# A list-scheduled two-layer encoder: other lengths for the loading queue in the plan

## The chip, the cores and the metric

The kernel runs on one core of one Trainium2 chip. The time is that of one execution on the device, in microseconds (us), the median of several runs. A core has TensorE (PE), VectorE (DVE), ScalarE (ACT), GpSimd (POOL) and SyncE (SP); SP only issues loads and copies. GpSimd and SP each have a queue of transfers, q0 and q1 in the profile, and 16 DMA engines serve both.

## The reference

A hybrid encoder of two layers in float32, 512 tokens of width 1024, feed-forward width 2816. Each layer runs four steps, every one closed by a layer norm:

```python
x = LN(alpha * x + 0.5 * swiglu(x, w_gate, w_up, w_down))   # first half feed-forward
x = LN(alpha * x + mixer_i(x))                              # token mixing
x = LN(alpha * x + mem_cross_attention(x, mem))             # 4 heads into 256 memory tokens
x = LN(alpha * x + 0.5 * swiglu(x, w_gate, w_up, w_down))   # second half feed-forward

def swiglu(x, w_gate, w_up, w_down):
    return (jax.nn.silu(x @ w_gate) * (x @ w_up)) @ w_down
```

mixer_0 (mixer_ab here) is one projection into two groups of heads, dense attention with rotary positions and attention in a window of 128 with a sink, and one output projection with ab_w_out. mixer_1 (mixer_c) is attention in a two-dimensional neighbourhood with a bias.

## The kernel before

Everything stays on the core from start to end: x is held as four tiles of 128 tokens (x0 to x3), and transposed as xh and xl for the matmuls. A product in float32 is made of three matmuls. Each operand is split into a high part (a cast on ScalarE) and a low part (a subtraction on VectorE), and high x high, high x low and low x high are added up in one PSUM bank. So a weight goes through four hands: a load of 512 KB or 1 MB on SP's or GpSimd's queue, a cast on ScalarE, a subtraction on VectorE, then matmuls on TensorE. In the trace "CAST slab<-slab" and "TENSOR_TENSOR slab<-slab,slab" are these two.

The stages follow each other: ffn0 (to about 330 us), mixer_ab (530), memory (750), ffn1 (1050), ffn2 (1390), mixer_c (1600), memory (1810), ffn3 (2130). The feed-forward steps go in groups of 512 hidden columns. In the groups that this text speaks of, the weights w_gate and w_up come in quarters and some products are taken of sums of quarters, which VectorE makes ("slab<-slab,slab ... f32<-"), so that a group needs fewer matmuls and more of VectorE.

The order of the instructions is not written by hand. The kernel's code is recorded as a graph of `Op` objects (`record`, from L138), each with an estimated time `ns`. `plan` (L181) plays the graph through a model of the five engines: at each step the engine that can start earliest takes its most urgent ready operation. Two lists in it, `queues`, model the loads: `begin`, `finish` and `lands` say when the first packet goes, when the last one has gone, and when readers may start. `plan` is called twice by `emit` (L298): from the first pass `deadlines` works out how late each operation may be, these become the keys of the second pass, and the operations are issued in the order of that pass.

Buffers are handed out in the same pass. Tiles of the kind slab share 27 buffers (t2: 14, raw: 2). A new tile gets the buffer that came free first in the model (`free`, a heap by time), and waits on the chip for the readers of the tile that had it before. The names in the orders below carry running numbers: slab_375 is a tile, not a buffer.

All instructions are issued by one helper line, L156, so every row of the profile names L156 (L157 after the change).

Of the kernel before, what the change touches and what calls it, by code (L numbers as in the profile page):

```python
# [39 lines left out]

class Op:
    __slots__ = (
        "engine", "adds", "ns", "call", "deps", "users", "wait", "ready", "end", "frees", "index", "rank", "dma", "size", "port", "table",
        "key", "start", "stop", "lands", "later",
    )

# [19 lines left out]
class Graph:  # L66
# [71 lines left out]
    def record(self, engine, method, args, kw):  # L138
        kw = dict(kw)
        aps = [z for z in list(args) + list(kw.values()) if hasattr(z, "tensor")]  # L140
        outs = [kw[k] for k in ("out", "accum_out") if k in kw]
        if "out" not in kw:
            outs.insert(0, args[0])
        ins = [z for z in aps if not any(z is o for o in outs)]
        op = Op()
        op.engine, op.index, op.dma, op.adds = engine, len(self.ops), method == "dma_start", "accum_op" in kw
        op.rank = op.index
        op.ns = self.cost(engine, method, outs[0], ins, kw)
        func = args[2] if method == "activation" else None
        op.table = str(func) if func in (AF.Silu, AF.Exp) else None  # L150
        op.size = math.prod(outs[0].shape) * 4
        op.port = method in ("tensor_tensor", "scalar_tensor_tensor", "tensor_scalar") and (
            engine == "gpsimd" or engine == "vector" and math.prod(outs[0].shape[1:]) >= 64 and all(z.space != bass.MemoryType.PSUM for z in ins)
        )
        fn = getattr(getattr(self.nc, engine), method)
        op.call = lambda: fn(*args, **kw)  # L156
        op.deps, op.users, op.frees, op.later = set(), [], [], []  # L157
        if self.after and engine in self.after[1]:
            op.deps.add(self.after[0])
        for z, writes in [(z, False) for z in ins] + [(z, True) for z in outs]:  # L160
            info = self.tiles.get(z.tensor.name)
            if info is None:
                continue
            p0, p1, runs = self.extent(z)
            opens = writes and kw.get("start", False)
            keep = []
            for q, w, a0, a1, other in info["log"]:
                over = opens or p0 < a1 and a0 < p1 and (
                    info["bank"] and q.engine != engine or any(l < b and a < h for l, h in runs for a, b in other)
                )  # L170
                if over and (w or writes or info["bank"] and q.engine != engine) and q is not op:
                    op.deps.add(q)
                covered = writes and p0 <= a0 and a1 <= p1 and all(any(l <= a and b <= h for l, h in runs) for a, b in other)
                if not covered:
                    keep.append((q, w, a0, a1, other))
            keep.append((op, writes, p0, p1, runs))
            info["log"] = keep
            info["users"].add(op)
        self.ops.append(op)

    def plan(self):  # L181

        for info in self.tiles.values():
            info["left"], info["at"], info["behind"] = len(info["users"]), 0.0, None
        now = {e: 0.0 for e in self.ENGINES}
        heaps = {e: [] for e in self.ENGINES}
        ready = {e: [] for e in self.ENGINES}
        free = {s: [(0.0, i, None) for i in range(s.bufs)] for s in self.spaces.values()}
        turn = {s: 0 for s in free}
        queues = {True: [(0.0, 0.0)], False: [(0.0, 0.0)]}  # L190
        held, order, table = [0.0, 0.0], [], None
        for op in self.ops:
            op.wait, op.ready = len(op.deps) + len(op.frees), 0.0

        def release(op, t):
            op.ready = max(op.ready, t)
            op.wait -= 1
            if op.wait == 0:
                heapq.heappush(heaps[op.engine], (op.ready, op.key, op.index, op))

        def grant(space):

            while turn[space] < len(space.queue) and free[space]:
                info = space.queue[turn[space]]
                turn[space] += 1
                if info["users"]:
                    t, _, info["behind"] = heapq.heappop(free[space])
                    for op in info["users"]:
                        release(op, t)

        def arrive(e):
            while heaps[e] and heaps[e][0][0] <= now[e]:
                _, key, i, op = heapq.heappop(heaps[e])
                heapq.heappush(ready[e], (key, i, op))

        for op in self.ops:
            if op.wait == 0:
                heapq.heappush(heaps[op.engine], (0.0, op.key, op.index, op))
        for space in free:
            grant(space)  # L220
        while len(order) < len(self.ops):
            best = None
            for e in self.ENGINES:
                arrive(e)
                if ready[e] and e in self.PATIENT:
                    key, _, op = ready[e][0]
                    for at, k, _, _ in heapq.nsmallest(4, heaps[e]):
                        if at < now[e] + op.ns * 0.6 and k < key - self.margin:
                            now[e] = at
                            arrive(e)  # L230
                            break
                if ready[e]:
                    t = now[e]
                elif heaps[e]:
                    t = heaps[e][0][0]
                else:
                    continue
                if best is None or t < best[0]:
                    best = (t, e)
            assert best, "no instruction can start"  # L240
            t, e = best
            if not ready[e]:
                now[e] = t
                continue
            _, _, op = heapq.heappop(ready[e])
            shared = lambda pairs, a, b: sum(max(0.0, min(b, y) - max(a, x)) for x, y in pairs)
            stop = t + op.ns
            if op.port:
                stop += max(0.0, held[e == "vector"] - t)
                held[e != "vector"] = stop  # L250
            if op.table and op.table != table:
                stop += 1290.0
                table = op.table
            lands = stop + self.LATENCY[e]
            if op.dma:
                kind = e == "sync"
                work = op.size / 2**19 * (4000.0 if op.adds else 1650.0)
                begin = max(stop + (1200.0 if kind else 2000.0), queues[kind][-1][1])
                finish = begin + work + 0.5 * shared(queues[not kind][-6:], begin, begin + work)
                queues[kind].append((begin, finish))  # L260
                lands = finish + 790.0
            op.start, op.stop, op.lands, now[e] = t, stop, lands, stop
            order.append(op)
            for u in op.users:
                release(u, stop if e == u.engine == "tensor" else lands)
            for info in op.frees:
                info["left"] -= 1
                info["at"] = max(info["at"], lands)
                if info["left"] == 0:
                    heapq.heappush(free[info["space"]], (info["at"], len(order), info))  # L270
                    grant(info["space"])
        return order
# [1388 lines left out]
```

## Time and profile before

| | us |
|---|---|
| median of three runs | 2132.85 |
| lowest and highest run | 2131.11, 2132.93 |
| profiled execution | 2131.03 |
| its span | 2129.3 |
| TensorE busy in it | 2112.0 |
| VectorE, ScalarE, GpSimd busy | 1735.8, 1161.7, 285.1 |

The granted clock of TensorE is 0.998 over the span. A row of the timeline has its start, its length, the engine, the line, the operation with the tiles that it writes and reads (without their numbers), how many instructions it sums up, and in brackets the idle time before it with what ended it. "PE" rows are matmuls; "a", "d" and "t" are PSUM banks, slab, raw and t tiles in the core's memory.

### The profile page before, as it was taken

The numbers are of one execution on the slowest core, as the hardware profiler recorded it, in microseconds if no ns is written. First come the engines' busy times: TensorE is split into PE (matmuls) and PEld (weight loads), VectorE is DVE, ScalarE is ACT, GpSimd is POOL, SyncE is SP. The second block draws the span as 40 slices with busy tenths as digits, with TensorE's granted clock in tenths as the row PEclk, the third lists the DMA queues.
The fourth block names the chain that finished last, engine by engine and source line by source line (L and its number), as shares of the span: only waits on it lengthen the run. The fifth ranks groups of instructions, "written<-read, shape, count | busy, mean of one in ns | idle before, by whom it ended". The sixth has DMA issues, their size and how long they took to land.

```text
span 2129.3 us, 32714 instructions
## 1 busy us (share of the span) xinstructions
PE 2112.0 (99%) x12648; PEld 1870.6 (88%) x12648; DVE 1735.8 (82%) x2500; ACT 1161.7 (55%) x1903; POOL 285.1 (13%) x379
## 2 busy tenths in 40 slices
PE   9999999999999999999999999999999999999997
PEld 7999988888888899998889999888888888999996
DVE  7789989888848879998879999866568479699997
ACT  5555443798546554445545455457665465444552
POOL 0001015310002000000200000312210011000003
PEclk9999999999999999999999999999999999999999
DMA  6566562003433346564445556256454433456551
GB/s 204 143 165 140 139 191 91 20 18 106 140 134 109 88 114 185 150 157 130 140 106 141 129 139 187 76 149 160 118 164 157 139 91 98 109 149 155 141 151 60
DMA packets 208859, 275.92 MB, mean 130 GB/s; under 512 B 10688, under 2 KB 151616, under 8 KB 208704
## 3 DMA queue, kind: packets, MB, share of 16 engines
q1 hardware_dynamic: 175904, 221.14, 33.6%
q0 software_dynamic: 32512, 52.44, 14.0%
q8 instruction: 100, 1.64, 0.3%
q14 instruction: 55, 0.45, 0.1%
q10 hardware_dynamic: 288, 0.26, 0.0%
HBM read 259.12 MB, written 4.19 MB: 124 GB/s over the span
## 4 chain that ended last, share of the span: by engine, by line
PE 89%; DVE 1%; DMA 1%; ACT 1%; issue 1%; SPq 0%; DVEq 0%; POOL 0%; ACTq 0%
PE a L156 55%; PE d L156 21%; PE t L156 14%; DMA slab<-t 1%; ACT slab L156 1%; DVE slab L156 1%; SPq L156 0%; DVE x L156 0%; ACT t L156 0%; DMA raw<-ab_w_out 0%; DVE t L156 0%; DVE xl L156 0%; DVEq L1657 0%; ACT xh L156 0%; DVE nmu L156 0%
## 5 line engine op out<-in xcount | busy, mean ns | idle before, releaser
L156 DVE TENSOR_TENSOR slab<-slab,slab 128x1024 fp32r<-128x1024 f32 (+3 forms) x638 | 727.9, 1167 | 76.0 <-ACT slab L156 37.7
L156 ACT CAST slab<-slab 128x1024 fp32r<-128x1024 f32 (+2 forms) x498 | 472.1, 983 | 341.4 <-DVE slab L156 142.7
L156 PE MATMUL a<-slab,slab 128*128 128x256 f32 (+3 forms) x2320 | 567.6, 323 | 1.9 <-DMA slab<-t 1.2
L156 PE MATMUL a<-xh,slab 128*128 128x256 f32 (+2 forms) x2480 | 559.8, 315 | 0.1
L156 PE MATMUL d<-slab,slab 128*128 128x512 f32 (+2 forms) x1856 | 447.8, 381 | 0.8 <-DVE slab L156 0.8
L156 PEld LDWEIGHTS a<-slab,slab 128*128 128x128 f32 x2320 | 409.4, 190 | 41.7 <-ACT t L156 1.3
L156 PEld LDWEIGHTS a<-xh,slab 128*128 128x128 f32 x2480 | 416.4, 190 | 33.4 <-ACT slab L156 1.0
L156 PE MATMUL a<-raw,slab 128*128 128x256 f32 x2048 | 388.8, 283 | 1.1 <-DVE t L156 1.0
L156 PE MATMUL a<-xl,slab 128*128 128x256 f32 (+1 forms) x1240 | 389.7, 314 | 0.0
L156 PEld LDWEIGHTS d<-slab,slab 128*128 128x128 f32 x1856 | 328.9, 189 | 57.2 <-DVE slab L156 1.7
L156 PEld LDWEIGHTS a<-raw,slab 128*128 128x128 f32 x2048 | 327.8, 192 | 6.7 <-ACT slab L156 1.9
L156 PEld LDWEIGHTS a<-xl,slab 128*128 128x128 f32 x1240 | 236.3, 191 | 18.4
L156 PE MATMUL t<-slab,slab 128*128 128x512 f32 (+1 forms) x840 | 209.3, 389 | 0.0
L156 DVE TENSOR_TENSOR slab<-raw,slab 128x1024 fp32r<-128x1024 f32 (+2 forms) x140 | 159.6, 1157 | 23.3 <-ACT slab L156 23.2
L156 PEld LDWEIGHTS t<-slab,slab 128*128 128x128 f32 x840 | 149.9, 189 | 26.2
L156 DVE TENSOR_TENSOR slab<-t,slab 128x512 fp32r<-128x512 f32 (+2 forms) x223 | 137.5, 637 | 12.3 <-ACT slab L156 11.2
L156 ACT CAST slab<-t 128x512 fp32r<-128x512 f32 (+2 forms) x223 | 120.7, 567 | 41.4 <-DVE t L156 15.0
L156 ACT CAST slab<-raw 128x1024 fp32r<-128x1024 f32 (+1 forms) x132 | 123.7, 970 | 25.1 <-PE a L156 9.0
L156 ACT COPY t<-a 128x512 f32<-128x512 f32 (+1 forms) x116 | 63.5, 551 | 130.0 <-PE a L156 76.5
L156 DVE SCALAR_TENSOR_TENSOR x<-d,x 128x512 f32<-128x512 f32 x168 | 114.9, 686 | 16.8 <-PE d L156 16.1
L156 POOL DMA_DIRECT2D slab<-ffn_w_down x40 | 47.7, 1193 | 315.2 <-DVE slab L156 296.9
L156 DVE TENSOR_TENSOR t<-a,t 128x512 f32<-128x512 f32 (+2 forms) x99 | 61.0, 618 | 33.8 <-PE a L156 20.6
(126 smaller groups left out, 2143.0 us busy)
## 6 DMA issues: line engine op xcount, KB each, us to landing
slab<-ffn_w_gate SPq DMA_DIRECT2D x80, 512.0 KB
slab<-ffn_w_up SPq DMA_DIRECT2D x80, 512.0 KB
slab<-ffn_w_down SPq DMA_DIRECT2D x80, 512.0 KB
slab<-ffn_w_down POOLq DMA_DIRECT2D x40, 512.0 KB, 5.8
raw<-mem_w_kv SPq DMA_DIRECT2D x16, 1024.0 KB
slab<-t SPq DMA_DIRECT2D x96, 128.0 KB
slab<-ffn_w_gate POOLq DMA_DIRECT2D x16, 512.0 KB, 7.7
slab<-ffn_w_up POOLq DMA_DIRECT2D x16, 512.0 KB, 6.0
```

What stands on the lines that cost most here:

```text
L156: op.call = lambda: fn(*args, **kw)
```

## The change

Only the planner's model of the loading queue is changed. A load on SP's queue of size bytes had a length of 1650 ns for each 512 KB; now it is 250 ns + 1700 ns for each 512 KB. Its first packet came 1200 ns after the end of the issue (`stop`), and the issue is modelled with a length of its own; now it comes 1040 ns after the start of the issue (`t`). A load of at least 512 KB on at most 64 partitions is marked `thin`, and its length is multiplied by 1.7: only the four pieces of ab_w_out for raw_1188 and raw_1193 are such. The accumulating loads on GpSimd's queue keep 4000 ns for each 512 KB, and other loads there 1650 ns.

```diff
@@ record
+        op.thin = op.dma and engine == "sync" and op.size >= 2**19 and outs[0].shape[0] <= 64
...
@@ plan
             if op.dma:
                 kind = e == "sync"
-                work = op.size / 2**19 * (4000.0 if op.adds else 1650.0)
-                begin = max(stop + (1200.0 if kind else 2000.0), queues[kind][-1][1])
+                work = 250.0 + op.size / 2**19 * 1700.0 if kind else op.size / 2**19 * (4000.0 if op.adds else 1650.0)
+                work *= 1.7 if op.thin else 1.0
+                begin = max(t + 1040.0 if kind else stop + 2000.0, queues[kind][-1][1])
                 finish = begin + work + 0.5 * shared(queues[not kind][-6:], begin, begin + work)
                 queues[kind].append((begin, finish))
                 lands = finish + 790.0
```

The instructions are the same; their order on the engines and the buffers of some tiles change. Three places, before and after; the bracket at the end of a row names the semaphores that it waits for.

VectorE in ffn0, at 113 us in the trace of before (slab_260 is a load, slab_217 a product for the next activation):

```order
L156 TENSOR_TENSOR slab_263<-slab_256,slab_262 128x1024 [waits DMAHW5_49,PE_49,Activation_49]
L156 TENSOR_TENSOR slab_266<-slab_265,slab_260 128x1024 [waits DMAHW6_49,DVE_49]
L156 TENSOR_TENSOR slab_217<-t_118_199,t_72_153 128x512
L156 TENSOR_TENSOR t_186_267<-slab_218,slab_217 128x512 [waits DVE_49]
L156 TENSOR_TENSOR t_187_268<-t_186_267,slab_217 128x512 [waits DVE_49]
L156 TENSOR_TENSOR slab_270<-slab_266,slab_269 128x1024 [waits PE_49,Activation_49]
```

The same rows of VectorE after the change:

```order
L157 TENSOR_TENSOR slab_263<-slab_256,slab_262 128x1024 [waits DMAHW5_49,PE_49,Activation_49]
L157 TENSOR_TENSOR slab_217<-t_118_199,t_72_153 128x512 [waits DVE_49]
L157 TENSOR_TENSOR slab_266<-slab_265,slab_260 128x1024 [waits DMAHW6_49,DVE_49]
L157 TENSOR_TENSOR t_186_267<-slab_218,slab_217 128x512 [waits DVE_49]
L157 TENSOR_TENSOR t_187_268<-t_186_267,slab_217 128x512 [waits DVE_49]
L157 TENSOR_TENSOR slab_270<-slab_266,slab_269 128x1024 [waits PE_49,Activation_49]
```

slab_217 has moved ahead of slab_266, the row that waits for a load (DMAHW6).

TensorE at the end of mixer_ab, at 527 us. slab_1189 to slab_1192 are the halves of one piece of ab_w_out (raw_1188), slab_1194 to slab_1197 those of the last piece (raw_1193); d_1199, a_1200 and d_1208 are the banks of three blocks of tokens:

```order
L156 MATMUL d_1199<-slab_1192,slab_1107 128x512
L156 MATMUL d_1199<-slab_1191,slab_1107 128x512
L156 MATMUL d_1199<-slab_1194,slab_1159 128x512 [waits Activation_49]
L156 MATMUL d_1199<-slab_1195,slab_1159 128x512 [waits DVE_49]
L156 MATMUL d_1199<-slab_1194,slab_1159 128x512
L156 MATMUL d_1199<-slab_1196,slab_1184 128x512 [waits Activation_49]
L156 MATMUL a_1200<-slab_1192,slab_1107 128x512
L156 MATMUL d_1199<-slab_1197,slab_1184 128x512 [waits DVE_49]
L156 MATMUL d_1199<-slab_1196,slab_1184 128x512
```

The same place on TensorE after the change:

```order
L157 MATMUL d_1199<-slab_1192,slab_1107 128x512
L157 MATMUL d_1199<-slab_1191,slab_1107 128x512
L157 MATMUL a_1200<-slab_1192,slab_1107 128x512
L157 MATMUL a_1200<-slab_1191,slab_1107 128x512
L157 MATMUL d_1208<-slab_1189,slab_1047 128x512 [waits DVE_49]
L157 MATMUL d_1199<-slab_1194,slab_1159 128x512 [waits Activation_49]
L157 MATMUL a_1200<-slab_1194,slab_1159 128x512
L157 MATMUL d_1208<-slab_1190,slab_1047 128x512
L157 MATMUL d_1208<-slab_1189,slab_1047 128x512
L157 MATMUL d_1208<-slab_1191,slab_1107 128x512
L157 MATMUL d_1208<-slab_1192,slab_1107 128x512
L157 MATMUL d_1199<-slab_1195,slab_1159 128x512 [waits DVE_49]
```

Matmuls of the other two blocks with the earlier piece (a_1200, d_1208) have moved ahead of and between those of d_1199 with the last piece.

SP's queue in a group of ffn0, from 156 to 184 us, and ScalarE at 179 us. slab_375 is the first quarter of the next group's w_up; this place recurs ten times over ffn0 to ffn3:

```order
L156 DMA slab_351<-ffn_w_down 128x2x512 [waits DMASW3_49,PE_49]
L156 DMA slab_367<-ffn_w_down 128x2x512 [waits DMAHW3_49,DVE_49,PE_49]
L156 DMA slab_375<-ffn_w_up 128x4x256 [waits DMAHW4_49,DVE_49,PE_49]
L156 DMA slab_378<-ffn_w_up 128x4x256 [waits DMAHW6_49,DMAHW5_49,DVE_49]
L156 DMA slab_379<-ffn_w_up 128x4x256 [waits DMAHW3_49,DVE_49]
```

ScalarE at the same place before:

```order
L156 COPY t_260_341<-a_346 128x512 [waits DVE_49,Activation_49]
L156 COPY t_261_342<-a_352 128x512 [waits PE_49]
L156 CAST slab_368<-slab_332 128x1024 [waits DMAHW6_49]
L156 CAST slab_371<-slab_367 128x1024 [waits DMAHW3_49,DVE_49,Activation_49]
L156 CAST slab_373<-slab_314 128x512 [waits PE_49]
```

SP's queue there after the change:

```order
L157 DMA slab_351<-ffn_w_down 128x2x512 [waits PE_49]
L157 DMA slab_367<-ffn_w_down 128x2x512 [waits DMAHW3_49,DVE_49,PE_49]
L157 DMA slab_375<-ffn_w_up 128x4x256 [waits DMASW5_49,DMAHW4_49,DVE_49,PE_49]
L157 DMA slab_378<-ffn_w_up 128x4x256 [waits DMAHW6_49,DMAHW5_49,DVE_49]
L157 DMA slab_379<-ffn_w_up 128x4x256 [waits PE_49]
```

ScalarE there after the change:

```order
L157 COPY t_260_341<-a_346 128x512 [waits DVE_49,Activation_49]
L157 CAST slab_368<-slab_332 128x1024 [waits DMAHW6_49,PE_49]
L157 COPY t_261_342<-a_352 128x512 [waits PE_49]
L157 CAST slab_371<-slab_367 128x1024 [waits DMAHW3_49,DVE_49,Activation_49]
L157 CAST slab_373<-slab_314 128x512 [waits PE_49]
```

On SP the loads keep their order. slab_375 has got another buffer, with a wait more (DMASW5, a load of long before), and its wait on PE is now for the last reader of slab_344, not of slab_349. On ScalarE the cast slab_368 and the copy of a_352 have changed places.

More of the change, by code (lines that the diff above doesn't have):

```diff
@@ L42 @@
     __slots__ = (
-        "engine", "adds", "ns", "call", "deps", "users", "wait", "ready", "end", "frees", "index", "rank", "dma", "size", "port", "table",
+        "engine", "adds", "ns", "call", "deps", "users", "wait", "ready", "end", "frees", "index", "rank", "dma", "size", "port", "table", "thin",
         "key", "start", "stop", "lands", "later",
```

## The prediction

> **What bounds the kernel now.** I read the page first, then the list of what TensorE waits for, then the timelines of each engine around every wait, and last the DMA queues in short windows. TensorE's row says nearly all:
>
> ```profile
> span 2129.3 us, 32714 instructions
> PE 2112.0 (99%) x12648; PEld 1870.6 (88%) x12648; DVE 1735.8 (82%) x2500; ACT 1161.7 (55%) x1903; POOL 285.1 (13%) x379
> ```
>
> TensorE is idle for 2129.3 - 2112.0 = 17.3 us. The change keeps all 12648 matmuls, so it can only move what lies in these 17.3 us. Where they lie:
>
> ```profile
> 2116.00:2129.30 13.30, 2.35 (x11) 1.59 (x9) 8.59 (x14) 1.24 (x2) 3.67 (x4) 0.74 0.50 158
> ...
> PE t L156 <- DVE junk L156: 1.2, 1, 1.2
> PE a L156 <- DMA slab<-t: 1.2, 3, 0.6
> ```
>
> The first row is the last 13.30 us, in which TensorE is busy for 2.35: 10.95 us are the end of the program (last normalisation and store), whose order on TensorE does not change. 1.2 us is the start. So 17.3 - 10.95 - 1.2 = 5.1 us are left in the middle, and that is the most that any order could bring back there. Adding idle time has no such limit.
>
> **The change part by part.** It removes and adds no instruction; it gives the planner other times for loads on SP's queue, and so moves rows on all five queues and hands some buffers to other tiles. I compared the two orders on each engine and went to each moved piece in the trace of before.
>
> *A wait in ffn0 at 129.8 us.* VectorE's row order changes at 113.8:
>
> ```profile
> 113.81 1.23 DVE L156 TENSOR_TENSOR slab<-slab,slab 128x1024 f32<-128x1024 f32 x1 [1.49 <-DMA slab<-ffn_w_down]
> 114.95 0.69 DVE L156 TENSOR_TENSOR slab<-t,t 128x512 f32<-128x512 f32 x1
> ...
> 123.15 2.96 DVE L156 TENSOR_TENSOR slab<-slab,slab 128x1024 fp32r<-128x1024 f32 x3 [0.20 <-ACT slab L156]
> ...
> 128.97 0.69 DVE L156 TENSOR_TENSOR t<-a,t 128x512 f32<-128x512 f32 x1
> ```
>
> ```profile
> 127.22 1.55 PE L156 MATMUL t<-slab,slab 128*128 128x512 f32 x6
> 129.80 0.36 PE L156 MATMUL a<-raw,slab 128*128 128x256 f32 x1 [1.03 <-DVE t L156]
> ```
>
> VectorE idles 1.49 us for a load (slab_266 reads slab_260), then runs almost without a gap to the t whose end at 129.66 lets TensorE go on at 129.80. The new order puts the 0.69 us product slab_217 into that idle time, ahead of the waiting instruction. All behind it comes up to 0.7 us sooner; the 0.20 of waiting for ScalarE at 123.15 may eat some. TensorE's wait is 1.03, so what goes is 0.65 (between 0 and 0.9), and what is late next is the same t, with 0.4 left.
>
> *The end of mixer_ab.* These weights are the ones on 64 partitions.
>
> ```profile
> 526.26 1.96 PE L156 MATMUL d<-slab,slab 128*128 128x512 f32 x7
> 528.98 0.98 PE L156 MATMUL d<-slab,slab 128*128 128x512 f32 x3 [0.76 <-DVE slab L156]
> ```
>
> ```profile
> 512.66 0.61 ACT L156 ACTIVATE t<-t,mn 128x385 f32<-128x385 f32 x1
> ...
> 514.14 1.19 ACT L156 CAST slab<-t 128x256 fp32r<-128x256 f32 x3 [0.28 <-PE t L156]
> ...
> 516.08 2.19 ACT L156 CAST slab<-raw 128x512 fp32r<-128x512 f32 x4
> ...
> 526.61 2.00 ACT L156 CAST slab<-raw 128x1024 fp32r<-128x1024 f32 x2 [1.98 <-DMA raw<-ab_w_out]
> ```
>
> The casts at 526.61 wait for the last piece of ab_w_out, VectorE's difference follows, and TensorE stops 0.76 us at d_1199<-slab_1195. Shown idle time starts at the modelled end of a matmul. Two 512-column matmuls in a row take 0.62 (the row at 374.57 further down) and six 1.55 (127.22), so one starts every (1.55 - 0.62) / 4 = 0.23 and lasts 0.39: against that pace the wait costs 0.76 + 0.39 - 0.23 = 0.92. Two things change. Between d_1199<-slab_1194 and d_1199<-slab_1195 now stand five other matmuls, and three more ahead of the first: 8 x 0.23 = 1.84 us more work, which covers the 0.92 alone. And the four casts of mem_t (516.08) move up to 512.66, three ahead of slab_1167's cast and the fourth soon behind, so that the buffer of raw_1193 comes free sooner. Against it: three of them take 3/4 of 2.19 = 1.64, so the cast that began at 514.14 begins at 514.31 at the earliest, and with what stands behind it TensorE meets two or three just-in-time casts later than before. I take +0.2 for that (0 to 0.6). Sum: -0.7, between -1.2 and -0.3.
>
> *mixer_c at 1530 us.* The "DMA slab<-t" in the list of waits is mostly this:
>
> ```profile
> 1529.53 0.25 PE L156 MATMUL a<-slab,slab 128*128 128x192 f32 x1
> 1530.38 0.33 PE L156 MATMUL a<-slab,slab 128*128 128x192 f32 x1 [0.60 <-DMA slab<-t]
> ```
>
> The first and second half of a_2886 stood back to back; the new order puts eight other matmuls between them, and at the 0.12 to 0.23 us of their pace that is over 1 us of work, so the wait of 0.60 goes. But the subtraction that frees the buffer of load raw_2909 now stands behind two more rows of VectorE, so that load is issued up to 1 us later, and these copies are behind it on SP's queue. The next matmul on that path (a_2892) gets VectorE's maximum behind a longer subtraction. I take -0.4 (-0.7 to +0.3).
>
> *mixer_ab at 374 us.* Here a wait is added:
>
> ```profile
> 368.38 0.74 POOL L156 TENSOR_TENSOR slab<-t,t 128x256 f32<-128x256 f32 x1
> ...
> 373.43 2.39 POOL L156 TENSOR_TENSOR slab<-t,t 128x512 f32<-128x512 f32 x1 [1.30 <-DVE t L156]
> ```
>
> ```profile
> 374.57 0.62 PE L156 MATMUL a<-slab,xh 128*128 128x512 f32 x2
> ```
>
> The transpose t_673 reads what GpSimd ends at 373.43 + 2.39 = 375.82. It stood eight matmuls further on and now stands at 374.57. GpSimd's 0.74 us product at 368.38 has moved behind the chain that feeds this, so the end comes at about 375.08: TensorE waits 0.5 us, with everything queued behind it (0 to 1.25, the upper end if GpSimd is no sooner).
>
> *The quarter loads of w_up.* Ten times (ffn0 to ffn3) the load of the first up quarter gets another buffer: not that of slab_349, last read by the matmul that ends at 179.74, but that of slab_344, last read five 512-column matmuls later. SP holds it for 5 x 0.23 = 1.15 us more, so it issues at 180.9 instead of:
>
> ```profile
> 179.77 4.33 SPq L156 DMA_DIRECT2D slab<-ffn_w_up  x3
> ```
>
> ```profile
> 185.51 1.05 ACT L156 CAST slab<-slab 128x1024 fp32r<-128x1024 f32 x1 [0.88 <-DMA slab<-ffn_w_up]
> ```
>
> ```profile
> 187.16 1.22 DVE L156 TENSOR_TENSOR slab<-slab,slab 128x1024 fp32r<-128x1024 f32 x1
> 188.30 0.69 DVE L156 TENSOR_TENSOR t<-a,t 128x512 f32<-128x512 f32 x1
> ```
>
> ScalarE waits for that landing, so at first sight this moves the path. The queues say otherwise. The next rows are bytes by queue, q0 GpSimd's and q1 SP's, in 180.9 to 183.1, in 183.6 to 187.4, and, at the last of the ten places, in 2017.8 to 2020.0:
>
> ```profile
> q0 software_dynamic: 190, 0.39, 107.3%
> ...
> q1 hardware_dynamic: 1383, 1.38, 108.2%
> ...
> q0 software_dynamic: 209, 0.43, 107.0%
> ```
>
> Until 183.1 not one packet of SP's moves: all 16 DMA engines are full with the down weights that GpSimd issued here:
>
> ```profile
> 178.37 1.20 POOL L156 DMA_DIRECT2D slab<-ffn_w_down  x1 [4.88 <-DVE slab L156]
> ```
>
> When nothing is in the way, the first packet comes 1.0 us after the issue (a load issued at 1742.96, forty slices of 0.1 us from there):
>
> ```profile
> 1742.96 0.37 SPq L156 DMA_DIRECT2D slab<-ffn_w_gate  x1
> ...
> DMA  0000000000873463689999999999888876978989
> ```
>
> An issue at 180.9 is ready at 181.9 and still waits until 183.1. The landing stays, and I cost the edit at 0. Its cover is the rest of the GpSimd transfer, 1.2 us; without it the whole 1.15 would come through.
>
> [...]
>
> *All other moved rows* (three matmuls at the start, single swaps in mixer_c and the layer starts, loads issued 1 to 2 us later whose readers come over 1.5 us after the landing): +0.2, between -0.5 and +1.0.
>
> Sum: -0.65 - 0.7 - 0.4 + 0.5 + 0 + 0.2 = -1.05 us. The profiled execution took 2131.03 (span 2129.3 and 1.7 around it), so it would take 2130.0. It is near the lowest of the three runs, 2131.11; the median is 2132.85, and from that the forecast is 2131.8.
>
> **The rivals.** *The up quarters land late, and it is slower.* If SP's packets do get in between, each of the ten landings is up to 1.15 later. At the first place VectorE (187.16) starts 0.60 after the cast ended (185.51 + 1.05), and its t (188.30 to 188.99) is 0.49 early for the matmul that reads it:
>
> ```profile
> 189.48 0.28 PE L156 MATMUL a<-raw,slab 128*128 128x256 f32 x1
> ```
>
> There 1.15 - 0.60 - 0.49 = 0.1 comes through. At the last place nothing is left over: the cast ends 2024.59, VectorE starts 0.03 later, and TensorE already starts late.
>
> ```profile
> 2023.54 1.05 ACT L156 CAST slab<-slab 128x1024 fp32r<-128x1024 f32 x1 [2.06 <-DMA slab<-ffn_w_up]
> ```
>
> ```profile
> 2024.62 1.23 DVE L156 TENSOR_TENSOR slab<-slab,slab 128x1024 fp32r<-128x1024 f32 x1 [0.53 <-ACT slab L156]
> ```
>
> There all 1.15 does. Ten places between 0.1 and 1.15, half-way 0.63: +6.3, so 2131.8 + 6.3 = 2138.1. It decides from the point where SP issues later than 183.1 - 1.0 = 182.1, and the new issue is 1.2 us short of that; or where the GpSimd transfer ends that much sooner. Against it stand the two windows without one SP packet. *The gains are given back.* TensorE pulled ahead by 0.7 meets its next just-in-time tile sooner; with 99% busy there are many such places. Then 129.8 and 528.98 shift instead of going, the added 0.5 at 374 and 0.2 elsewhere stay: 2132.85 + 0.7 = 2133.6. *The new times for loads do nothing useful*, rows merely swap: 2132.85; this counts with the second. *All goes well*: every middle wait that is touched vanishes, nothing is added: -0.9 - 1.2 - 0.7 - 0.5 = -3.3, 2129.6.
>
> **How the numbers follow.** My forecast, a small gain with its terms near the values taken, 0.55. Given back or nothing, 0.28. Late up quarters, 0.10. All well or better, 0.04; some load or buffer that I did not see and that costs over 4 us, 0.03. 0.2% of 2132.85 is 4.27 us, about what a measurement of this kernel can tell from no change; all cases but the late quarters and the unseen one lie within it. Faster by that much would need nearly all of the 5.1 us: 0.03. Slower: 0.10 of the late quarters and 0.02 of the unseen: 0.12. Within: 0.85. The range goes from the best sum, 2129.6, less 0.3 for the scatter of the runs, 2129.3, up past the second rival and half of the terms' upper ends to 2135.6, and leaves the slower rival out.
>
> **What would show it.** In the profile after: TensorE's wait near 129.8 at about 0.4; none at d_1199<-slab_1195; none for slab<-t near 1530; a new one of 0.5 for GpSimd near 374.6; the up quarters issued 1.15 later after their matmuls and landing, against the GpSimd transfer, at the same time; busy time unchanged at 2112. I am wrong if the idle sum leaves 14.5 to 19 us, or if ScalarE's cast near 185.5 comes a microsecond later and TensorE waits behind it ten times.

## The result, and the profile after

The changed kernel takes 2127.38 us (median of 11 runs, 2125.79 to 2128.19) against 2132.05 (11 runs, 2129.83 to 2133.01): a ratio of 0.9978, 95% interval 0.9970 to 0.9986. It is faster by about 4.7 us, where 2131.8 was forecast and 2129.3 was the low end of the range. The two profiled executions stand at 2131.03 and 2126.97. The page after:

```profile
span 2125.2 us, 32740 instructions
PE 2110.4 (99%) x12648; PEld 1870.4 (88%) x12648; DVE 1736.4 (82%) x2500; ACT 1161.4 (55%) x1903; POOL 288.0 (14%) x379
```

TensorE's idle time fell from 17.3 to 14.8 us, by 2.5, and its busy time from 2112.0 to 2110.4, by 1.6. The matmuls are the same, so I take the second part as waiting too, counted as busy where the modelled end of a matmul lies behind the next start (a 512-column matmul is shown 0.39 long, and in a run one starts every 0.23). The lateness below, taken from the starts alone, falls by 4.11, as much as both parts together. The end of the program is what it was (15.20 - 4.24 = 10.96 us idle, as before 10.95):

```profile
2110.00:2125.20 15.20, 4.24 (x19) 3.10 (x17) 10.25 (x15) 2.37 (x4) 4.37 (x4) 0.74 0.44 139
```

What TensorE still waits for (total, times, longest):

```profile
PE t L157 <- DVE junk L157: 1.2, 1, 1.2
PE t L157 <- DVE x L157: 0.8, 2, 0.7
PE a L157 <- DMA slab<-t: 0.6, 2, 0.3
PE a L157 <- DVE slab L157: 0.4, 1, 0.4
```

VectorE's wait at 129.8 and its subtraction at 528.98 are off the list. The three waits for copies "slab<-t" (1.2) are gone as well; the two now listed (0.6) stand at other places, 0.32 at 1458.74 and 0.25 at 1503.80. To see where the 4 us went I summed TensorE's *lateness*: for each matmul the time from its start to the next start, less the pace that rows of its width keep in a run (0.227 us for 512 columns, 0.120 for 256, 0.113 for 192). It has no modelled end in it. A stretch is cut at the same counts of matmuls in each kernel and is named by its time in the kernel before:

```
stretch, us              before   after
0 to 100 (start)           2.68    2.48
100 to 150 (ffn0)          1.44    0.26
150 to 490                 5.11    5.26
490 to 579 (mixer_ab)      2.54    1.69
579 to 1475               7.66    7.48
1475 to 1607 (mixer_c)     4.67    2.95
1607 to the last matmul    2.60    2.47
sum                       26.71   22.60
```

Three stretches carry 3.75 of 4.11 us. In ffn0 VectorE's product now fills the idle time and, in addition, the load behind it is there at once:

```profile
112.56 0.68 DVE L157 TENSOR_TENSOR slab<-t,t 128x512 f32<-128x512 f32 x1
113.16 1.22 DVE L157 TENSOR_TENSOR slab<-slab,slab 128x1024 f32<-128x1024 f32 x1
...
127.58 0.69 DVE L157 TENSOR_TENSOR t<-a,t 128x512 f32<-128x512 f32 x1
```

The t that TensorE waited for starts at 127.58 instead of 128.97 (the prediction shows the rows of before). At the end of mixer_ab the matmuls run on where the wait of 0.76 stood, with a small new one 8 us later:

```profile
527.68 1.75 PE L157 MATMUL d<-slab,slab 128*128 128x512 f32 x7
...
536.18 1.09 PE L157 MATMUL t<-ident,x 128*128 128x128 f32 x8 [0.18 <-DVE x L157]
```

In mixer_c two waits for copies that the prediction did not show stood in the kernel before (0.44 and 0.51 lost against the pace, less of it shown):

```profile
1482.86 0.58 PE L156 MATMUL a<-slab,slab 128*128 128x192 f32 x3 [0.28 <-DMA slab<-t]
...
1552.90 0.33 PE L156 MATMUL a<-slab,slab 128*128 128x192 f32 x1 [0.30 <-DMA slab<-t]
```

They are gone, and so is the one at 1530. Where the first stood, the rows after run without a gap, and the new wait comes 24 us later:

```profile
1479.60 0.86 PE L157 MATMUL a<-slab,slab 128*128 128x192 f32 x6
1480.29 1.46 PE L157 MATMUL d<-slab,slab 128*128 128x256 f32 x10
...
1503.80 0.33 PE L157 MATMUL a<-slab,slab 128*128 128x192 f32 x1 [0.25 <-DMA slab<-t]
```

### The profile page after: what moved, and what is told of

Read it like the earlier page. It is cut to its first block, busy times and chain, and to the rows that moved or that the text cites. A ratio compares the mean times of both kernels' runs of the same rounds, so it can differ in the third digit from the quotient of the medians.

```text
span 2125.2 us, 32740 instructions
## 1 busy us (share of the span) xinstructions
PE 2110.4 (99%) x12648; PEld 1870.4 (88%) x12648; DVE 1736.4 (82%) x2500; ACT 1161.4 (55%) x1903; POOL 288.0 (14%) x379
## 3 DMA queue, kind: packets, MB, share of 16 engines
q8 instruction: 100, 1.64, 0.3%
## 4 chain that ended last, share of the span: by engine, by line
PE 97%; DVE 1%; DMA 1%; ACT 1%; issue 0%; SPq 0%; POOL 0%; DVEq 0%; ACTq 0%
PE a L157 59%; PE d L157 23%; PE t L157 15%; DVE x L157 0%; DMA slab<-t 0%; DVE slab L157 0%; DMA raw<-mem_w_kv 0%; SPq L157 0%; ACT slab L157 0%; ACT t L157 0%; DMA raw<-x_t 0%; DVE t L157 0%; ACT xh L157 0%; ACT junk L157 0%; POOL lny L157 0%
## 5 line engine op out<-in xcount | busy, mean ns | idle before, releaser
L157 ACT ACTIVATE t<-a 128x512 f32<-128x512 f32 (+3 forms) x65 | 36.3, 559 | 89.7 <-PE a L157 89.7
```

## The experiments

Times below stand beside runs of the kernel before on the same chip. Their intervals are about 0.0009 of the time to each side, 1.9 us, so single pieces of about 1 us are read from the lateness of one profile of each kernel. Lateness scatters as well: in the seven kernels whose rows in mixer_c are those of before it is 3.97 to 5.89, mean 4.94; in the three with the new rows 2.55 to 3.29, mean 2.93. In ffn0 the twelve with the old rows have 1.13 to 1.64, mean 1.37.

**Early half, late half.** The new lengths hold only on one side of a time in the plan:

```diff
+                new = t < 1390e3
+                work = 250.0 + op.size / 2**19 * 1700.0 if kind and new else op.size / 2**19 * (4000.0 if op.adds else 1650.0)
+                work *= 1.7 if op.thin and new else 1.0
+                begin = max((t + 1040.0 if new else stop + 1200.0) if kind else stop + 2000.0, queues[kind][-1][1])
```

> The new model of the loading queue only while the planner's clock is below 1390 us, so the orders up to the end of ffn2 are those of the changed kernel and the rest is as before. Theory (the gain is a sum of local ones, each where a wait of TensorE goes, and what is won stays won): TensorE's lateness against a steady pace falls by 1.2 in 100 to 150 us and by 0.9 in 500 to 550, and the time by 2.1 us in all (ratio 0.9990), about half of the whole change's 4.07. Rival 1 (what is won early is given back at the next tile that comes just in time, and only mixer_c's part counts): the early waits go and others grow behind them, time within 0.5 us of before. Rival 2 (one place opens the way for all, the early lead makes the later waits go): about the whole 4 us, the waits at 1482 to 1553 smaller although their order is unchanged.

Measured: 2130.07 beside 2131.73, ratio 0.9992 (0.9984 to 1.0001). ffn0 0.84, the end of mixer_ab 1.30 (-0.60 and -1.24), mixer_c 5.26. Its profile also has a wait of 1.1 at 1365 that other kernels with the old rows show or don't show; the last section shows the same wait in another kernel. The two gains are local, and rival 2 is out: mixer_c is no better with its old rows. Rival 1 is not excluded by this run alone. The 1.1 and the 0.6 more in mixer_c offset the gains, so that the sum over the profile is that of before (26.5 beside 26.7), and the interval of the time includes no change; both offsets also occur in kernels with the old order.

The other half has the same edit with `t >= 1390e3`.

> The complement: the new model only from 1390 us on, so mixer_c, ffn3 and the end stand in the new order and all ahead of them as before. Theory (local and additive): the waits near 1482.9, 1485.1, 1530.4, 1552.3 and 1552.9 go, one of about 0.4 appears near 1505, and the time falls by 2.0 us (ratio 0.9991), although the prediction had put only -0.4 there. Rival 1 (only mixer_c's part counts): -4. Rival 2 (the early lead makes the later waits go): these waits stay, and the time is within 0.5 us of before.

Measured: 2130.77, ratio 0.9994 (0.9985 to 1.0003). mixer_c falls to 3.29, all five waits named are gone (two others, 1.1 in all, stand at 1572 and none at 1505), and ffn0 (1.38) and mixer_ab (2.52) are as before. By the lateness the late half brings its share without the early lead, so the two halves are separate gains; the median alone (-1.0, with 1.9 to each side) would not show it. The prediction had all of mixer_c at -0.4 and +0.2.

**Which of the three numbers.** Only the line with 1.7:

```diff
                 work = op.size / 2**19 * (4000.0 if op.adds else 1650.0)
+                work *= 1.7 if op.thin else 1.0
```

> Of the three parts of the change only the factor of 1.7 for large loads on 64 partitions. Its order differs from that before only at the end of mixer_ab. Theory: TensorE's wait at d_1199<-slab_1195 near 529 goes, lateness in 500 to 550 us falls by 0.9 (a wait of up to 0.3 may come a few us later), the time by 0.8 us (ratio 0.9996). Rival (the gain there comes from the loads ahead of it that the other two parts moved): the wait stays, 0 +- 0.3.

Measured: 2130.23, ratio 0.9992 (0.9984 to 1.0001). The wait at d_1199 is gone and the lateness at the end of mixer_ab is 0.93 instead of 2.54, which is more than the theory had. And the change without that line:

> The change without the factor of 1.7: the sooner first packet and the longer transfers only. Its order is that of the changed kernel except at the end of mixer_ab. Theory: all of the gain but that at the end of mixer_ab, so 4.07 - 0.8 = 3.3 us less than before (ratio 0.9985), and a wait of 0.7 to 1.0 near 528 that the changed kernel does not have. Rival (the factor brings most): within 1 us of before.

Measured: 2128.74, ratio 0.9983 (0.9975 to 0.9992); mixer_ab 2.39, ffn0 0.18, mixer_c 2.55. The wait is back:

```profile
527.72 0.97 PE L157 MATMUL d<-slab,slab 128*128 128x512 f32 x3 [0.71 <-DVE slab L157]
```

So the factor of 1.7 makes the gain in mixer_ab, and the other two numbers together make the rest; no run takes these two apart.

**ffn0, one row.** On VectorE alone:

```diff
- slab_266<-slab_265,slab_260 128x1024
  slab_217<-t_118,t_72 128x512
+ slab_266<-slab_265,slab_260 128x1024
```

> Before, with one row moved: VectorE's product slab_217 ahead of the sum slab_266 that waits for a load, in ffn0. Theory (the product fills the idle time, and all behind it comes up to 1.3 us sooner, less what the load's own landing differs): TensorE's wait at 129.8 falls from 1.2 to between 0 and 0.6, time -0.9 us (ratio 0.9996). The prediction's step: -0.65, a wait of 0.4 to 0.5 left. Rival (the wait goes through other rows that the change moved, such as loads): 0, the wait stays at 1.0 or more.

Measured: 2131.67 beside 2132.66, ratio 0.9994 (0.9985 to 1.0003); ffn0 0.89, the wait left is

```profile
129.67 0.36 PE L157 MATMUL a<-raw,slab 128*128 128x256 f32 x1 [0.48 <-DVE t L157]
```

That is the "0.4 left" of the prediction: its step holds, in this one profile, for the row that it looked at. In that kernel the load of slab_260 lands 7.66 us after its issue (before 7.69), in the changed kernel 6.79. Four swaps more, as in the change:

```diff
 VectorE
- slab_232<-slab_170,slab_231
  slab_233<-slab_127,slab_233
+ slab_232<-slab_170,slab_231
- slab_245<-slab_234,slab_244
  slab_246<-slab_234,slab_235
+ slab_245<-slab_234,slab_244
...
 ScalarE: the casts slab_231 and slab_269 one row later
```

> Before, with five swaps in ffn0 as in the changed kernel: on VectorE slab_217 ahead of slab_266, slab_232 behind slab_233 and slab_245 behind slab_246, on ScalarE the casts of slab_231 and slab_269 one row later. Theory (slab_217 alone was worth 0.4 of the 1.06 that wait is worth on average; the rest is that the load of slab_260 lands 0.6 to 0.9 us sooner after its issue, since slab_232 one row later holds GpSimd's load of slab_234 back by 0.3): the load of slab_260 takes 6.8 to 7.1 us from issue to landing instead of 7.7, the wait at 129.8 is between 0 and 0.3, time -0.9 us. Rival (the sooner landing comes from rows before 100 us): 7.7 again, and a wait of 0.6 as with slab_217 alone.

Measured: 2131.93 beside 2132.80, ratio 0.9997 (0.9988 to 1.0006); the load takes 6.85 us, ffn0 is 0.18 and the wait is gone. The sooner landing is more than scatter: with the new rows the load takes 6.79 to 7.11 us in the four kernels that have them, and 7.22 to 7.82 in the other thirteen. The reason given for it fails: GpSimd's load of slab_234 was issued 0.63 us ahead of SP's load of slab_260, just as before (105.02 and 105.65; before 105.39 and 106.02). In the changed kernel it is 0.34 ahead (105.47 and 105.81), with about the same landing. Why these swaps make the load land sooner stays open. It does not always clear the wait: the kernel with the early half has this order and a landing after 7.11, and 0.42 of the wait is left.

**The wait at 374 that did not come.** One matmul moved:

```diff
+ t_673<-ident,slab_613 128x128
  ...
- t_673<-ident,slab_613 128x128
```

> Before, with one matmul moved: the transpose t_673 eight rows earlier on TensorE, as in the changed kernel, while GpSimd and VectorE keep the order of before. Theory (the wait of 0.5 that the prediction added here did not come because GpSimd's product ended at 372.65 instead of 375.82: two of its rows moved behind it, and it took 1.30 instead of 2.39 since it no longer ran beside VectorE's subtraction of slab_711): here it still ends at 375.8, so TensorE waits 1.1 to 1.4 us at about 374.6, time +1.2 us (ratio 1.0006). Rival (the wait would have been hidden anyway, TensorE having other slack there): below 0.3.

Measured: 2133.66 beside 2132.80, ratio 1.0004 (0.9995 to 1.0013), and in the profile a wait of 1.28 against the pace, shown as 1.12:

```profile
373.33 2.37 POOL L156 TENSOR_TENSOR slab<-t,t 128x512 f32<-128x512 f32 x1 [1.30 <-DVE t L156]
...
375.75 0.33 PE L156 MATMUL t<-ident,slab 128*128 128x128 f32 x1 [1.12 <-POOL slab L156]
```

In the changed kernel the same product is done before TensorE comes to it. VectorE's subtraction, which starts with it in the kernel before, starts 0.97 after it (the row of before first):

```profile
373.48 1.21 DVE L156 TENSOR_TENSOR slab<-raw,slab 128x1024 fp32r<-128x1024 f32 x1
```

```profile
371.35 1.30 POOL L157 TENSOR_TENSOR slab<-t,t 128x512 f32<-128x512 f32 x1 [0.70 <-DVE t L157]
...
372.32 1.42 DVE L157 TENSOR_TENSOR slab<-raw,slab 128x1024 fp32r<-128x1024 f32 x1
```

```profile
373.26 0.28 PE L157 MATMUL t<-ident,slab 128*128 128x128 f32 x1
```

The matmul's move alone costs 1.3 us of lateness; in the changed kernel GpSimd's earlier product, shorter in its new place, pays for it.

**The price of late up quarters.** On SP's queue, at ten places:

```diff
- slab_375<-ffn_w_up
  slab_378<-ffn_w_up
+ slab_375<-ffn_w_up
```

> Before, with ten pairs of loads on SP's queue exchanged: the load of the first up quarter (slab_375 and its nine counterparts) behind the load of the next one. Its issue and its landing come some 1.5 us or more later. It prices the prediction's slower rival. If these landings are on the path as that rival had it, at the first place 1.5 - 0.60 - 0.49 = 0.4 comes through and at the last all 1.5: ten places between 0.4 and 1.5, 4 to 15 us slower, half-way 9.5 (ratio 1.0045). If they are not: within 1 us of before.

Measured: 2148.11 beside 2132.80, ratio 1.0074 (1.0062 to 1.0087), five runs: 15 us slower, the top of what was expected. At the first place the quarter landed at 188.24 instead of 185.49, 2.75 later and not 1.5, and TensorE waits:

```profile
188.26 2.00 ACT L157 CAST slab<-slab 128x1024 fp32r<-128x1024 f32 x2 [3.66 <-DMA slab<-ffn_w_up]
```

```profile
191.32 0.36 PE L157 MATMUL a<-raw,slab 128*128 128x256 f32 x1 [1.71 <-DVE t L157]
```

The rival's price was real; 2.75 - 0.60 - 0.49 = 1.66 by the prediction's own slack, 1.71 shown. Its condition, that the quarters land late in the changed kernel, did not come.

**mixer_c: by engine.** The new rows from 1390 us on, on TensorE alone, and then on all the others alone.

> Every engine in the order of before, except that TensorE's rows from 1390 us on (mixer_c and later) stand in the new order. Theory (two mechanisms: at 1482.9 and 1485.1 the wait goes because the copies themselves come sooner, which the other engines' rows do; at 1530.4, 1552.3 and 1552.9 it goes because TensorE has other ready matmuls in between): lateness in 1450 to 1500 us nearly as before (-0.3 to 0), the waits at 1530 and 1552 gone, sum about -1.1 us (ratio 0.9995). Rival 1 (TensorE's own order does all of it): -1.8, the waits at 1482.9 and 1485.1 gone too. Rival 2 (the feeding engines do all of it): 0, all five waits stay.

Measured: 2132.25 beside 2132.66, ratio 0.9999 (0.9990 to 1.0008), mixer_c 5.16.

> The complement: from 1390 us on VectorE, ScalarE, GpSimd and SP's queue stand in the new order, TensorE in that of before. Theory: lateness in 1450 to 1500 us falls by 1.2, the waits near 1530 and 1552 stay (0.7 and 0.7, or a little longer where a load is issued later), sum about -1.0 us (ratio 0.9995). Rival 1 (TensorE's own order does all): 0. Rival 2 (the feeding engines do all): -1.8.

Measured: 2133.76, ratio 1.0004 (0.9995 to 1.0013), mixer_c 6.09. Neither half of the rows shows a gain: together they are worth 2.0, alone nothing that stands out of the scatter (6.09 is just above the 5.89 of the old rows). Both rivals, which had -1.8 in one of the halves, fall. Of the theory one part is seen: with TensorE's order alone no wait for copies is listed any more from 1500 to 1607. Waits of TensorE for VectorE stand there instead (0.38 at 1507 and 0.20 at 1530), and 1495 to 1522 rises from 0.5 to 1.0. What stands at 1482 in each, TensorE's order first, then the others':

```profile
1482.72 0.59 PE L157 MATMUL a<-slab,slab 128*128 128x192 f32 x3 [0.72 <-DMA slab<-t]
1484.55 0.51 PE L157 MATMUL d<-slab,slab 128*128 128x256 f32 x2 [0.29 <-DVE t L157]
```

```profile
1484.72 0.47 PE L157 MATMUL a<-slab,slab 128*128 128x192 f32 x2 [0.35 <-DVE mn L157]
1487.16 0.47 PE L157 MATMUL a<-slab,slab 128*128 128x192 f32 x2 [0.29 <-DVE mn L157]
```

With TensorE's order alone the copies are still late; with the others' alone the copies are in time and TensorE stops two microseconds further on, for VectorE, which has yet to take the maxima ("mn") from the bank.

**mixer_c: one tile, then its neighbours.** The rows that make slab_2722 stand ahead of the last reader of raw_2740, and so hold up the load of raw_2790 and the copies behind it on SP. Moved alone (ScalarE's cast and VectorE's subtraction):

```diff
- slab_2722<-t_2640
  slab_2666<-t_2645
  slab_2743<-raw_2740 (VectorE: slab_2744)
  slab_2780<-raw_2779
+ slab_2722<-t_2640
```

> Before, with two rows moved: ScalarE's cast and VectorE's subtraction that make slab_2722 stand behind those of slab_2780 (and so behind slab_2744's subtraction, the last reader of raw_2740, whose buffer the load of raw_2790 takes). Theory (the moved row frees that buffer sooner; the load is issued 0.3 to 0.6 us sooner, and the copies slab<-t behind it on SP's queue land up to 1 us sooner): the wait at 1482.9 falls from 0.44 by 0.3 or more, lateness in 1450 to 1500 us by 0.4 to 1.2, the time by as much. Rival (the copies come sooner for another reason, such as the bias loads on GpSimd's queue, which the new order moves too): 0 +- 0.2 there.

Measured: 2131.91, ratio 0.9995 (0.9986 to 1.0004). The load of raw_2790, first before and then here:

```profile
1474.05 0.37 SPq L156 DMA_DIRECT2D raw<-c_w_in  x1
```

```profile
1474.79 0.37 SPq L157 DMA_DIRECT2D raw<-c_w_in  x1
```

The last matmul of d_2745 starts at 1481.72 and 1482.87, so the load is issued 8.08 us ahead of it instead of 7.67, and the last copy of slab_2730 lands 0.03 after it instead of 1.00: the mechanism is there. The time is not: lateness in 1475 to 1495 is 1.65 (before 1.26, the seven with old rows 1.26 to 2.08), since TensorE stops further on:

```profile
1485.60 0.33 PE L157 MATMUL a<-slab,slab 128*128 128x192 f32 x1 [0.60 <-DVE mn L157]
1486.54 0.33 PE L157 MATMUL a<-slab,slab 128*128 128x192 f32 x1 [0.24 <-DMA slab<-t]
```

Then with the 24 matmuls that put the readers of slab_2731 behind ready work:

> Before, with only the rows around 1482 us in the new order, on both sides: the cast and subtraction of slab_2722 behind those of slab_2780 and the subtraction of slab_2781 earlier (they let the copies of slab_2730 land 1 us sooner), and 24 matmuls of TensorE, in which the readers of slab_2731 stand behind ready matmuls of d_2775 and d_2776. Theory (a chain of two waits: sooner copies of slab_2730 take away the first, and TensorE then meets the copies of slab_2731, which only its own new order covers; either alone moved nothing): lateness in 1450 to 1500 us falls from 2.3 to 1.1..1.5, the time by 0.8 to 1.2 us (ratio 0.9995). Rival (other rows are needed too, such as the bias loads and GpSimd's sums): lateness there stays over 2.0.

Measured: 2132.48 beside 2132.80, ratio 1.0001 (0.9992 to 1.0010), lateness in 1475 to 1495 1.32. One wait is left, a bank of PSUM that VectorE's row for t_2666 has yet to read:

```profile
1486.82 0.51 PE L156 MATMUL d<-slab,slab 128*128 128x256 f32 x2 [0.42 <-DVE t L156]
```

And with that row ahead of the maxima:

> As the kernel with the rows around 1482 us on both sides, and one row more: VectorE's reading of d_2745 (it makes t_2666) stands ahead of the four maxima and not behind two of them, as in the changed kernel. Theory (three waits in a row on one path: copies of slab_2730, copies of slab_2731, and then d_2776, which takes the bank of d_2745 and so waits for its reader; each is hidden behind the one before it, so that any two of the three edits move nothing): lateness of TensorE in 1450 to 1500 us is 1.0 to 1.5 instead of 2.3 to 2.7, the time 0.9 to 1.2 us less (ratio 0.9995). Rival (the other moved rows, GpSimd's bias loads and sums among them, are needed as well): 1.9 or more.

Measured: 2132.94 beside 2133.34, ratio 0.9998 (0.9989 to 1.0007). No wait is left between 1479 and 1490; of the 0.95 in 1475 to 1495, 0.48 is a wait ahead of the place, at 1477.4. So each edit laid bare the next wait, and with the three the place is clear. But 1522 to 1540 has 1.65 (before 1.18, the old rows at most 1.22), and mixer_c in all 4.85: in this profile the gain is gone 45 us later.

**mixer_c: by place.** All engines' new rows up to 1500 us, or from there on.

> Of the new order from 1390 us on, all engines' rows up to 1500 us; behind them the order of before. Theory (joint over the engines at one place, additive over the places): lateness in 1450 to 1500 us 1.0 to 1.4 (before 2.3), in 1500 to 1700 us as before, 3.4 to 4.4; time -1.1 us (ratio 0.9995). Rival (TensorE, ahead by 1.1, gives it back at 1530 or 1552): lateness in 1500 to 1700 us grows to 5.

Measured: 2132.97, ratio 0.9998 (0.9990 to 1.0007). 1475 to 1495 has 0.47, as in the changed kernel (0.37). But 1522 to 1540 has 1.25 and 1540 to 1607 2.62 (before 1.77), mixer_c in all 4.80. The gain at 1482 is there, and in this profile the rest grows by about as much, as the rival had it. That the one causes the other is not shown: a kernel with the old rows, the one with late up quarters, has 2.59 in 1540 to 1607. The wait at 1530 is still there:

```profile
1530.29 0.33 PE L156 MATMUL a<-slab,slab 128*128 128x192 f32 x1 [0.52 <-DMA slab<-t]
```

> The complement: all engines' rows of the new order from 1500 us on, in front of them the order of before. Theory: lateness in 1450 to 1500 us as before, 2.3 to 2.7; in 1500 to 1700 us 2.9 to 3.7 instead of about 4.1, the wait at 1530 gone; time -0.8 us (ratio 0.9996). Rival (the later gain needs the earlier rows): no change in 1500 to 1700 us.

Measured: 2134.16, ratio 1.0003 (0.9995 to 1.0012). 1475 to 1495 has 1.73, 1522 to 1540 0.47, the wait at 1530 is gone, but 1495 to 1522 rises to 0.99 (before 0.47); mixer_c in all 4.63. By lateness this is what the theory expected (3.62 in 1500 to 1700, 2.57 in 1450 to 1500), but the old rows alone give 3.3 to 5.0 and 2.3 to 2.7 there. Whatever part of the new order was taken, in seven kernels, mixer_c stayed between 4.13 and 6.09; only the whole of it comes to 2.55 to 3.29. Against the mean of the old rows, 4.94, the two parts by place bring 0.14 and 0.31, and the whole 2.01. Since the same rows scatter between 3.97 and 5.89, one profile of each part does not decide whether the places depend on each other or the parts' gains were hidden.

## Why the prediction was wrong, step by step

*What bounds the kernel:* the end of the program is unchanged. But the 5.1 us of idle time in the middle are not all that an order can bring back: of the 4.1 us only 2.5 came out of idle time, and 1.6 out of busy time, which was to stay at 2112 and is 2110.4. So the idle sum of 14.8 stayed within the 14.5 to 19 named as the sign of being right, while the time left its range. *The start value:* 2132.85 was the median of three runs; that of eleven is 2132.05, so 0.8 of the 4.4 us between forecast and result is not the change.

*ffn0, -0.65:* the twelve old and three new profiles (0.26, 0.18, 0.84) differ by 0.94. The term was right for its row and short by what the other swaps bring with the sooner load.

*End of mixer_ab, -0.7:* the wait went. The fourteen profiles with the old rows have 2.39 to 2.77, mean 2.56, the three with the new ones 0.93, 1.30 and 1.69, mean 1.31: -1.25. The +0.2 for more just-in-time casts did not come.

*374, +0.5:* did not come. The step that failed here is the 2.39 us taken for GpSimd's product. Against the matmul that waits, it starts 0.77 sooner (371.35 and 373.26; before 373.43 and 374.57), as the prediction's 0.74 had it. With 2.39 it would have ended at 373.74, 0.48 late, which is the +0.5; it takes 1.30 at its new time, where VectorE's subtraction starts 0.97 after it and not 0.05, and ends at 372.65.

*mixer_c at 1530, -0.4,* and *all other moved rows, +0.2:* this is the step that decided, two terms mis-sized: -0.2 for all of mixer_c, where its rows are worth -2.0 (4.94 to 2.93). I priced the one wait whose two matmuls I saw move apart (0.74 against the pace) and put the four others (0.44 and 0.27 near 1483, 0.21 and 0.51 near 1552) among "single swaps", with a small loss. All five go in the changed kernel and in the one with the late half alone; against the pace they make 2.17. Each of these waits lies where TensorE, VectorE and ScalarE are all rearranged, and the block could have been followed through as one, wait after wait, ahead of the result. Why no part of the order shows its share in mixer_c as a whole stays open.

*Quarter loads, 0:* right, and for the reason given. Taking out the 1.37 us by which all is earlier, SP issues 1.15 later (179.55; before 179.77), and the quarter lands 1.51 us behind the landing of GpSimd's transfer in both kernels (182.16 and 183.67; before 183.98 and 185.49). GpSimd's issue is 0.6 sooner, so it even lands 0.45 sooner. In the profile after, from SP's issue at 179.55 to 181.2, not one packet of SP's moves, and GpSimd's take 111.5% of the 16 engines' time; before, the first window of the prediction had 107.3%.

*The rivals:* "given back" was at 0.28. It did not come in the whole; in parts of the change 1.65 and 2.62 behind 1482 look like it, without showing it. "All goes well" had -3.3 at 0.04. It came out 0.8 (by lateness) to 1.4 (by the medians) better than that, since that sum took 0.7 for 1530 and 0.5 for all others. The misses add up: 0.3 in ffn0, 0.55 in mixer_ab, 0.5 at 374 and 1.8 in mixer_c, 3.15 beyond the -1.05; that makes -4.2, beside -4.06 of the two profiles.

## What to carry to other kernels

When a planner moves rows on all engines around one place, go through every wait of that place, and price the block as a whole. Behind the wait that you see gone the next one stood at 1482 (copies, then maxima that free a bank, then the next copies, then a bank again), and it took three edits to clear the place. In mixer_c as a whole seven partial versions of the order showed no gain beyond the scatter, and the whole order brought 2.0. That a wait taken away among just-in-time copies is a gain only when the next place is in step with it fits these runs, but is not shown. And idle time is not the whole of what an order can win: 1.6 of the 4.1 us stood in the profile as busy.

## Of the hardware, not expected

At two places an instruction of VectorE's or GpSimd's is shown longer by 1.1 to 2.4 us. At 1362 a subtraction of VectorE's, of a form that takes 1.22 us at 187.16, takes 2.40 in the profile before, and 3.64 in that of the kernel with slab_2722 moved, whose rows there are the same; TensorE then waits 0.95. First before, then that kernel:

```profile
1362.64 2.40 DVE L156 TENSOR_TENSOR slab<-slab,slab 128x1024 fp32r<-128x1024 f32 x1
```

```profile
1360.14 9.01 POOL L156 TENSOR_TENSOR x<-x,slab 128x512 f32<-128x512 f32 x6
```

```profile
1362.76 3.64 DVE L157 TENSOR_TENSOR slab<-slab,slab 128x1024 fp32r<-128x1024 f32 x1
```

```profile
1360.26 5.05 POOL L157 TENSOR_TENSOR x<-x,slab 128x512 f32<-128x512 f32 x4
1367.08 3.00 POOL L157 TENSOR_TENSOR x<-x,slab 128x512 f32<-128x512 f32 x2 [1.77 <-DVE x L157]
```

```profile
1367.14 1.17 PE L157 MATMUL t<-slab,slab 128*128 128x512 f32 x4 [0.95 <-DVE x L157]
```

Four sums of GpSimd in a row take 5.05, 1.26 each. VectorE's subtraction is 1.18 over 1.22 in the first and 2.42 over it in the second: 1.24 from the one to the other, about one of these sums. And the product at 374 takes 2.39 where a subtraction of 1.21 starts 0.05 after it, and 1.30 where the subtraction starts 0.97 after it. That the two engines wait for whole instructions of each other is my estimate from these lengths; no run shows how, nor what decides which of the two takes longer: at 373 GpSimd's recorded start is 0.05 ahead of VectorE's, and GpSimd's product is the long one. Nine of the seventeen profiles have this 1.1 us at 1365, whatever their order; neither of the pair before and after has it. Three of the nine have another 1.2 near 1426, and the start scatters as well (2.23 to 4.04 of lateness in the first 100 us). Two profiles of this kernel can differ by 2 us with no cause in the change.
